# Half of the contraction of three projection groups moved into the start of a diffusion backbone

## The chip, the cores and the metric

The kernel runs on one core of a Trainium2 chip. The metric is the device time of one execution in microseconds (us). The median of three runs of the kernel before is 2949.97 us (2944.76 to 2962.67). A profiled execution, from which every row below comes, took 2949.88 us; its span, from the first to the last instruction of the program, is 2947.9 us.

## The reference, cut to what matters

A two-layer backbone works on 256 latent tokens and 256 context tokens of width 2048, all in float32. Only the beginning of the first layer concerns us:

```
sh1, sc1, ... = split(silu(c) @ ada_w[0] + ada_b[0], 6)          # the same with c_ctx for the context
h  = rmsnorm(x)   * norm_mix[0] * (1 + sc1)  + sh1               # 256 x 2048, "modulation"
hc = rmsnorm(ctx) * norm_mix[0] * (1 + csc1) + csh1
ka, va, kb, vb, a, b, qa, qb, za = split(h  @ ev_w_in[0])        # input projection
ka, va, kb, vb, a, b            = split(hc @ ev_w_in[0])         # context: the first six alone
ka, va, qa = silu(short convolution over tokens, 5 taps)
y = [ gated delta rule(qa, ka, va, a, b, za) , neighbourhood attention(qb, kb, vb) ] @ ev_w_out[0]
x = x + g1 * y
```

The gated delta rule (GDN) splits time into chunks of 64, solves a small triangular system in each, and carries a state over the chunks: first over the context, then over the latent tokens. After it come the feed-forward part of layer 0, a layer with a short gated convolution, and its feed-forward part. `ka`, `va` and `qa` are 1024 columns wide each.

## The kernel before, in words

**Precision.** Each weight tile `raw` is split into `whi` (rounded, on ScalarE) and `wlo` (the rest; 576 of 1024 columns on VectorE, the others on GpSimd). The activations are split in the same way, and each product is three matmuls: hi x hi, lo x hi, hi x lo.

**Streams.** `fm_stream` computes 512 columns of the projection as four groups `f` of 128 columns, for the latent (256) and the context (256) tokens, in four PSUM banks; it goes over the 16 blocks `k` of the contraction (128 each). One step is one `k`: for each `f`, three products for each of the two token sets, 24 matmuls of 256 columns. In the very first step two of them are joined to one of 512 columns, from a tile `h0` in which latent and context lie side by side. Weights come two `k` at a time, 512 KB per DMA from SyncE's queue (`load_w`, L230); four raw tiles and two pairs of split tiles rotate. `grouped` holds back the matmuls of the last two steps (`TAIL`) so that each `f` ends, and is evacuated, while the next still runs. Seen as a generator, a stream gives control back after each step.

**The start.** The shift and the scale of the first modulation take 33.5 MB of `ada_w`. They come in eight blocks `b` of 256 columns (`start_block`: four DMAs of 1 MB in eight issues, 16 products with the conditioning vector, L484). `start_tokens(b)` copies the result (`mrow`, L490), turns it (L495), forms shift and scale, transposes the normalised tokens (L192), modulates (L508), and splits into `h_hi`, `h_lo` (L509, L510) for `k` = 2b and 2b+1. After each of the first seven blocks two steps of the first stream are traced: columns 0 to 511 of `ka`, called KA0 here. It has its last two steps after the eighth block.

**What follows.** KA1 (`ka` 512 to 1023), the gates (a, b), the chunk matrices and the triangular solve of the context, QA0 and QA1, VA0 and VA1, then the scans over the context and the latent tokens, with the streams of `qb`, `kb`, `vb` and `za`, neighbourhood attention, and the output projection (WO). Evacuating a KA, VA or QA stream (`head_evac`) copies the four sums to `hst` tiles (four buffers), and queues the convolution of each `f` (`conv_silu`: ScalarE and four taps on VectorE, L563), the transposes and the norm as work that later steps pop, one item per step (`later`, `drive`). The result goes to DRAM (`kd` by L630) and is read by the GDN part.

**Other vectors.** A `Pump` feeds the remaining `ada_w` products of layer 0 (`ada_job`, 192 steps of 256 KB, L330 and L338) between the steps of the streams: one per KA1 step, 0.5 per QA, 0.8 per VA, 0.6 per QB, 1.3 per KB, VB and ZA, 1.0 per WO step. Sixteen steps make a block of 512 columns, twelve blocks three vectors; a block's products are added up on VectorE (three of four) and on ScalarE and GpSimd, then summed over the partitions by TensorE in a small PSUM tile (L345). The last of them, the scale `sc` of the feed-forward part (L363), is used by the norm after WO (L1185).

**Order.** The program is traced in this order, but a planner places the instructions on each engine when the program is built: it simulates the time line and lets an instruction that is ready go ahead of one that was traced earlier and isn't. On the chip each engine then follows its list, and SyncE's queue is a list too.

Of the kernel before, what the change touches and what calls it, by code (L numbers as in the profile page):

```python
# [26 lines left out]
OP = mybir.AluOpType  # L27
# [3 lines left out]
KT = D // 128  # L31
FH = 5632
# [77 lines left out]
def body(tc, x, c, ctx, c_ctx, ada_w, ada_b, norm_mix, norm_ffn, ffn_w_gate, ffn_w_up, ffn_w_down,  # L110
# [186 lines left out]
    def fm_stream(segs, ks, ws, evac, cut=None):  # L297

        ps = [None] * 4
        for i, group in grouped(((k, (k, hi, lo)) for k, hi, lo in w_steps(segs, ks, cut)), len(ks)):  # L300
            for f in range(4):
                if i == 0:
                    ps[f] = mmt()
                for g, (k, hi, lo) in enumerate(group):
                    a, b = hi[:, f * 128:(f + 1) * 128], lo[:, f * 128:(f + 1) * 128]
                    if i == 0:
                        PE.matmul(ps[f][:, 0:len(ws) * 256], a, h0[:, 0:len(ws) * 256], start=True, stop=False)
                    for j, (wt, mv) in enumerate(((a, h_hi), (a, h_lo), (b, h_hi))):
                        for n, w in enumerate(ws):
                            if j or i:  # L310
                                PE.matmul(ps[f][:, n * 256:(n + 1) * 256], wt, mv(w, k), start=False,  # L311
                                          stop=i == len(ks) - 1 and g == len(group) - 1 and j == 2 and w == ws[-1])
                if i == len(ks) - 1:
                    evac(f, ps[f])
            yield
# [108 lines left out]
    h0 = hlp.tile([128, 512], F32R, name="h0")  # L424
    hs_hi = (hlp.tile([128, KT - 1, 256], F32R, name="hlhi"), hcp.tile([128, KT - 1, 256], F32R, name="hchi"))
    hs_lo = (hlp.tile([128, KT, 256], F32R, name="hllo"), hcp.tile([128, KT, 256], F32R, name="hclo"))

    def h_hi(w, k):
        return hs_hi[w][:, k - 1, :] if k else h0[:, w * 256:(w + 1) * 256]
# [8 lines left out]

    st = Stack()
# [48 lines left out]
    def start_tokens(b, pr):  # L488
        mrow = sp.tile([128, 512], F32, name="mrow", tag="mrow", bufs=2)
# [12 lines left out]
        for k in range(2 * b, 2 * b + 2):  # L502
# [3 lines left out]
            for w in range(2):  # L506
                m = sp.tile([128, 256], F32, name="modt", tag="modt", bufs=4)
                ACT.activation(m, p[:, w * 256:(w + 1) * 256], AF.Identity, bias=sh0[:, k, w:w + 1], scale=sc0[:, k, w:w + 1])  # L508
                DVE.tensor_copy(h_hi(w, k), m)  # L509
                DVE.tensor_tensor(h_lo(w, k), m, h_hi(w, k), op=OP.subtract)  # L510

    def token_stats():
# [5 lines left out]
        junk = sp.tile([128, D], F32, name="junk")  # L518
# [49 lines left out]
    def head_evac(n, q, c0, done, sums):  # L568
# [58 lines left out]
    def ka_evac(q):  # L627
# [3 lines left out]
        return head_evac(4, q, 0, done, True)  # L631

    def va_evac(q):
        def done(vt, ss):
            ACT.dma_start(hslice(vd_, 0, 4, q), vt.rearrange("p t h e -> p t (h e)"))
        return head_evac(4, q, 8, done, False)
# [25 lines left out]
    rstk = Stack()  # L662
# [13 lines left out]
    drive(fm_stream([(wv, C_KA + 512, 512)], ks, [0, 1], ka_evac(1)), pump, R_KA)  # L676
# [80 lines left out]
    state = gw.tile([128, 2, 8, 128], F32, name="state")  # L757
# [94 lines left out]
    def inverses(parts, q):  # L852
# [7 lines left out]
        xdT = gw.tile([128, 16, 128], F32, name="xdT", tag="xdT", bufs=XDT)  # L860
# [113 lines left out]
    for q in range(2):  # L974
        drive(fm_stream([(wv, C_VA + q * 512, 512)], ks, [0, 1], va_evac(q)), pump, R_VA)
# [50 lines left out]

    for q in range(2):
# [372 lines left out]
```

## Time and profile before

| | |
|---|---|
| median of three runs | 2949.97 us (2944.76 to 2962.67) |
| profiled execution, its span | 2949.88 us, 2947.9 us |
| TensorE (PE) busy, mean granted clock | 2764.4 us (94%), 0.978 |
| VectorE (DVE) busy | 1901.8 us (65%) |
| ScalarE (ACT) busy | 1337.0 us (45%) |
| GpSimd (POOL) busy | 596.2 us (20%) |
| read and written in HBM | 657.63 MB and 20.48 MB |

The page gives each engine's busy time, and its share of each of 40 equal slices of the span. A view by windows gives the same for stretches that the reader names, each number with the count of instructions in brackets, then the clock that was granted to TensorE, the busy share of the DMA engines and what they moved. The time line lists instructions as start, duration, engine, line, operation, output<-inputs, with the idle time of the engine ahead of it and what ended that in square brackets. A matmul's end is modelled: the pace is read from the distance between the starts of two of them.

### The profile page before, as it was taken

How to read it: one execution, taken by the hardware profiler on the slowest of the kernel's cores; microseconds unless marked ns; L12 is line 12 of the kernel's file. 1: busy time of each engine (PE TensorE's matmuls, PEld its weight loads, DVE VectorE, ACT ScalarE, POOL GpSimd, SP SyncE). 2: the span in 40 equal slices, each digit the busy share in tenths (PEclk: the TensorE clock that was granted, in tenths of full speed). 3: DMA queues.
4: the chain of work that ended last, by engine and by line, in shares of the span. 5: the costliest groups of instructions: out<-in, count | busy, mean ns of one | idle time of the engine just before them, and what ended most of it. 6: DMA issues, size and time to landing. Idle time of an engine off the chain costs nothing. (4 is left out here: it accounts for less than half of the span.)

```text
span 2947.9 us, 40712 instructions
## 1 busy us (share of the span) xinstructions
PE 2764.4 (94%) x15113; PEld 2295.6 (78%) x15113; DVE 1901.8 (65%) x2409; ACT 1337.0 (45%) x1822; POOL 596.2 (20%) x431
## 2 busy tenths in 40 slices
PE   6998888989899899999999998899999999999997
PEld 3697888978777778888878777777778888888886
DVE  2378786744457777666777767777767546445675
ACT  3245444333355444544445555344454444444554
POOL 1157535335241111100111101111111001000010
PEclk9998999999999999999999999999999999999999
DMA  9955657765657688877778766878658657656553
GB/s 343 289 162 160 185 177 251 232 205 184 180 155 262 236 298 294 293 266 270 268 273 274 252 204 234 285 268 297 211 177 315 199 184 257 188 182 220 192 192 123
DMA packets 284930, 680.82 MB, mean 231 GB/s; under 512 B 57273, under 2 KB 97313, under 8 KB 283323
## 3 DMA queue, kind: packets, MB, share of 16 engines
q1 hardware_dynamic: 262148, 652.48, 66.6%
q10 hardware_dynamic: 22583, 25.73, 2.9%
q8 instruction: 119, 1.95, 0.3%
q14 instruction: 80, 0.66, 0.1%
HBM read 657.63 MB, written 20.48 MB: 230 GB/s over the span
## 5 line engine op out<-in xcount | busy, mean ns | idle before, releaser
L241 DVE TENSOR_TENSOR wlo<-raw,whi 128x1024 fp32r<-128x1024 f32 (+1 forms) x800 | 998.0, 1260 | 530.7 <-ACT whi L173 499.2
L173 ACT ACTIVATE whi<-raw 128x1024 fp32r<-128x1024 f32 x800 | 835.8, 1056 | 668.0 <-PE mm L285 479.4
L338 DVE SCALAR_TENSOR_TENSOR acc<-araw,cT,acc 128x1024 f32<-128x1024 f32 (+1 forms) x312 | 366.5, 1175 | 248.7 <-DMA araw<-in_ada_w_dram 222.3
L283 PE MATMUL mm<-wlo,fhi 128*128 128x512 f32 x1232 | 477.7, 393 | 2.1 <-DVE wlo L241 2.0
L282 PE MATMUL mm<-whi,fhi 128*128 128x512 f32 x1232 | 475.9, 397 | 0.0
L285 PE MATMUL mm<-whi,flo 128*128 128x512 f32 x1232 | 392.4, 392 | 0.0
L336 POOL TENSOR_TENSOR acc<-araw,acc 128x1024 f32<-128x1024 f32 (+1 forms) x78 | 159.0, 2039 | 1068.6 <-ACT araw L335 599.5
L283 PEld LDWEIGHTS mm<-wlo,fhi 128*128 128x128 f32 x1232 | 232.4, 189 | 53.7 <-DVE wlo L241 5.0
L285 PEld LDWEIGHTS mm<-whi,flo 128*128 128x128 f32 x1232 | 231.6, 188 | 50.6
L282 PEld LDWEIGHTS mm<-whi,fhi 128*128 128x128 f32 x1232 | 232.7, 189 | 48.4
L282 PE MATMUL mm<-whi,ahi 128*128 128x512 f32 x672 | 262.3, 395 | 4.0 <-DVE rtmp L1157 2.9
L283 PE MATMUL mm<-wlo,ahi 128*128 128x512 f32 x672 | 261.9, 393 | 0.2 <-DVE wlo L241 0.2
L243 POOL TENSOR_TENSOR wlo<-raw,whi 128x448 fp32r<-128x448 f32 x112 | 163.4, 1460 | 285.7 <-ACT whi L173 267.3
L285 PE MATMUL mm<-whi,alo 128*128 128x512 f32 x672 | 211.7, 395 | 2.8 <-DVE alo L177 2.6
L335 ACT ACTIVATE araw<-araw,cT 128x1024 f32<-128x1024 f32 (+1 forms) x78 | 74.4, 954 | 256.3 <-DMA araw<-in_ada_w_dram 235.2
L311 PE MATMUL mm<-hllo,whi 128*128 128x256 f32 x640 | 184.1, 293 | 0.0
L311 PE MATMUL mm<-hlhi,wlo 128*128 128x256 f32 x600 | 168.3, 296 | 14.1 <-DVE wlo L241 10.6
L311 PE MATMUL mm<-hlhi,whi 128*128 128x256 f32 x600 | 170.4, 296 | 5.8 <-ACT whi L173 4.2
L1159 POOL TENSOR_TENSOR xs<-rtmp,xs 128x512 f32<-128x512 f32 x24 | 35.4, 1493 | 633.2 <-DVE rtmp L1157 631.9
L282 PEld LDWEIGHTS mm<-whi,ahi 128*128 128x128 f32 x672 | 127.0, 189 | 32.9 <-issue 3.4
L285 PEld LDWEIGHTS mm<-whi,alo 128*128 128x128 f32 x672 | 126.2, 189 | 32.7 <-DVE alo L177 5.7
L283 PEld LDWEIGHTS mm<-wlo,ahi 128*128 128x128 f32 x672 | 126.8, 189 | 29.5 <-DVE wlo L241 2.0
(398 smaller groups left out, 4694.0 us busy)
## 6 DMA issues: line engine op xcount, KB each, us to landing
araw<-in_ada_w_dram SPq DMA_DIRECT2D x288, 512.0 KB
raw<-in_ffn_w_down_dram SPq DMA_DIRECT2D x176, 512.0 KB
raw<-in_ffn_w_gate_dram SPq DMA_DIRECT2D x160, 512.0 KB
raw<-in_ffn_w_up_dram SPq DMA_DIRECT2D x160, 512.0 KB
raw<-in_ev_w_in_dram SPq DMA_DIRECT2D x112, 512.0 KB
araw<-in_ada_w_dram SPq DMA_DIRECT2D x192, 256.0 KB
raw<-in_od_w_in_dram SPq DMA_DIRECT2D x96, 512.0 KB
raw<-in_ev_w_out_dram SPq DMA_DIRECT2D x32, 512.0 KB
```

Source lines behind the costliest of these rows:

```text
L173: ACT.activation(dst, src, AF.Copy)
L241: DVE.tensor_tensor(lo[:, 0:cut], raw[:, 0:cut], hi[:, 0:cut], op=OP.subtract)
L243: POOL.tensor_tensor(lo[:, cut:], raw[:, cut:], hi[:, cut:], op=OP.subtract)
L282: PE.matmul(ps[ti][n], a, hi[:, n * 512:(n + 1) * 512], start=first, stop=False)
L283: PE.matmul(ps[ti][n], a, lo[:, n * 512:(n + 1) * 512], start=False, stop=False)
L285: PE.matmul(ps[ti][n], b, hi[:, n * 512:(n + 1) * 512], start=False, stop=last)
L311: PE.matmul(ps[f][:, n * 256:(n + 1) * 256], wt, mv(w, k), start=False, stop=i == len(ks) - 1 and g == len(group) - 1 and j == 2 and w == ...
L335: ACT.activation(raw, raw, AF.Copy, scale=col)
L336: POOL.tensor_tensor(acc2, raw, acc2, op=OP.add)
L338: DVE.scalar_tensor_tensor(acc, raw, col, acc, op0=OP.mult, op1=OP.add)
L1159: eng.tensor_tensor(v, tmp, v, op=OP.add)
```

## The change

Three streams are cut in two along the contraction: the first eight `k`, and the last eight. VA0's first half and KA1's first half (`half`) are traced in the start, ahead of KA0. Their sums are copied from PSUM to two SBUF tiles `part` (2 x 1 MB, 8 KB of a partition each); when the second half has run, `head_evac` adds `part` on VectorE in place of the copy. KA0 keeps its 16 steps in one accumulation. Of the three streams 24 steps are traced in the blocks 0 to 6, as 2, 2, 2, 6, 4, 4 and 4, where KA0 had 14 as 2 each; KA0 has eight steps after the eighth block, KA1 and VA0 eight each in their old places.

The two `part` tiles take the places of `state` and of one `xdT` buffer of the GDN part, whose pool (`xp`) now opens before the start. To make room, `mrow` has one buffer in place of two, `modt` three in place of four, and `junk` lies in `hs_lo`. A second tile in which latent and context lie side by side (`lead[8]`) serves the first step of the second halves.

```diff
@@ fm_stream
-                        PE.matmul(ps[f][:, 0:len(ws) * 256], a, h0[:, 0:len(ws) * 256], start=True, stop=False)
+                        PE.matmul(ps[f][:, 0:len(ws) * 256], a, lead[k][:, 0:len(ws) * 256], start=True, stop=False)
...
-    h0 = hlp.tile([128, 512], F32R, name="h0")
+    lead = {k: hlp.tile([128, 512], F32R, name=f"h{k}") for k in (0, KH)}      # KH = 8
...
+    rstk = Stack()
+    xp = pool("sums", stack=rstk, side="right")
...
-        mrow = sp.tile([128, 512], F32, name="mrow", tag="mrow", bufs=2)
+        mrow = sp.tile([128, 512], F32, name="mrow", tag="mrow", bufs=1)
...
-                m = sp.tile([128, 256], F32, name="modt", tag="modt", bufs=4)
+                m = sp.tile([128, 256], F32, name="modt", tag="modt", bufs=3)
...
-        junk = sp.tile([128, D], F32, name="junk")
+        junk = hs_lo[0][:, 0:KH, :].rearrange("p k t -> p (k t)")
...
@@ head_evac
-            copy(st_[i_], p[:, 0:n * 128])
+            if part is None:
+                copy(st_[i_], p[:, 0:n * 128])
+            else:
+                DVE.tensor_tensor(st_[i_], p, part[:, i_, :], op=OP.add)
...
+    def half(c0, tag, **kw):
+        part = xp.tile([128, 4, 512], F32, name="part", tag=tag, **kw)
+        return part, fm_stream([(wv, c0, 512)], ks[:KH], [0, 1], lambda f, p: copy(part[:, f, :], p))
...
+    part_va, sv_ = half(C_VA, "state")
+    part_ka, sk_ = half(C_KA + 512, "xdT", bufs=XDT)
     s0 = fm_stream([(wv, C_KA, 512)], ks, [0, 1], ka_evac(0))
+    plan = [s for s, n in ((sv_, KH), (sk_, KH), (s0, KH)) for _ in range(n)]
     for b in range(8):
         start_tokens(b, sums)
         if b < 7:
-            next(s0), next(s0)
+            for _ in range((2, 2, 2, 6, 4, 4, 4)[b]):
+                next(plan.pop(0))
             sums = start_block(b + 1)
+    for s in plan:
+        next(s)
...
-    drive(fm_stream([(wv, C_KA + 512, 512)], ks, [0, 1], ka_evac(1)), pump, R_KA)
+    drive(fm_stream([(wv, C_KA + 512, 512)], ks[KH:], [0, 1], ka_evac(1, part_ka)), pump, R_KA)
...
-    for q in range(2):
-        drive(fm_stream([(wv, C_VA + q * 512, 512)], ks, [0, 1], va_evac(q)), pump, R_VA)
+    drive(fm_stream([(wv, C_VA, 512)], ks[KH:], [0, 1], va_evac(0, part_va)), pump, R_VA)
+    drive(fm_stream([(wv, C_VA + 512, 512)], ks, [0, 1], va_evac(1)), pump, R_VA)
```

More of the change, by code (lines that the diff above doesn't have):

```diff
@@ L31 @@
 KT = D // 128
+KH = KT // 2
 FH = 5632
@@ L566, in conv_silu, with head_evac @@
         return o
-    def head_evac(n, q, c0, done, sums):
+    def head_evac(n, q, c0, done, sums, part=None):
         st_ = {}
@@ L756, in body @@
     flush()
-    state = gw.tile([128, 2, 8, 128], F32, name="state")
     def g4(name, tag, bufs=1):
```

18 lines of the change are left out of this document (10 added, 8 removed).

## The prediction

> **What bounds the kernel now.** I read the page first, for the share of TensorE and for the slices in which it is not full.
>
> ```profile
> PE 2764.4 (94%) x15113; PEld 2295.6 (78%) x15113; DVE 1901.8 (65%) x2409; ACT 1337.0 (45%) x1822; POOL 596.2 (20%) x431
> ...
> PE   6998888989899899999999998899999999999997
> ```
>
> TensorE is busy 94% of the span, so the same work placed elsewhere gains only what idle time, or half-speed time, it fills. One slice is 74 us. The first is thin, and slices 4 to 10 (220 to 740 us) are at 8 as often as at 9. The view by windows, cut where a block of the start turns (L495) and where the first matmuls of KA1 (146.10), QA0 (204.40) and QB0 (406.70) stand, says what is thin there.
>
> ```profile
> 44.57:80.03 35.46, 32.89 (x257) 23.43 (x253) 11.21 (x32) 7.03 (x11) 5.12 (x3) 1.00 1.09 353
> 80.03:136.83 56.80, 51.68 (x385) 35.50 (x385) 17.71 (x52) 12.17 (x20) 7.74 (x6) 0.94 0.95 309
> 136.83:146.10 9.27, 8.10 (x64) 7.61 (x65) 4.28 (x13) 3.37 (x7) 3.03 (x2) 1.00 0.66 172
> 146.10:204.40 58.30, 55.86 (x462) 54.69 (x461) 47.99 (x59) 24.98 (x34) 36.86 (x29) 1.00 0.49 150
> 204.40:300.00 95.60, 81.47 (x592) 78.54 (x591) 79.15 (x140) 51.66 (x80) 61.90 (x55) 0.89 0.52 165
> 300.00:406.70 106.70, 96.44 (x773) 94.40 (x773) 90.76 (x171) 45.84 (x72) 55.50 (x57) 0.97 0.55 165
> ```
>
> The columns are window, length, then busy time of PE, its weight loads, DVE, ACT and POOL, the granted clock, the share of the DMA engines and GB/s. In the start (rows one to three) the DMA engines are full, at 353 GB/s, and TensorE is nearly full as well: 51.68 of 56.80 us from the turn of block 3 (80.03) to that of block 7 (136.83). The three rows after are KA1, then QA with the first GDN matrices, then VA with the triangular solve. There VectorE is busy 217.9 of 260.6 us, and TensorE idles 2.4, 14.1 and 10.3 us. So the start, where the change works, has little room, and the stage from which it takes work has more holes.
>
> The time line of TensorE shows the holes of the start themselves.
>
> ```profile
> 82.33 1.06 PE L484 MATMUL gd<-araw,cT 128*32 128x512 f32 x8 [0.23 <-DMA araw<-in_ada_w_dram]
> 88.92 0.28 PE L311 MATMUL mm<-hlhi,wlo 128*128 128x256 f32 x1
> 89.04 0.28 PE L311 MATMUL mm<-hchi,wlo 128*128 128x256 f32 x1
> 92.44 1.07 PE L484 MATMUL gd<-araw,cT 128*32 128x512 f32 x8 [1.27 <-DMA araw<-in_ada_w_dram]
> 94.42 1.84 PE L495 MATMUL sm<-cs,mrow 128*128 128x2 f32 x8 [0.91 <-DVE mrow L490]
> 97.14 1.94 PE L484 MATMUL gd<-araw,cT 128*32 128x512 f32 x8
> 136.83 1.02 PE L495 MATMUL sm<-cs,mrow 128*128 128x2 f32 x8 [0.91 <-DVE mrow L490]
> 137.71 1.18 PE L192 MATMUL sm<-cs,xn 128*128 128x128 f32 x8
> 140.06 0.74 PE L311 MATMUL mm<-hlhi,whi 128*128 128x256 f32 x4 [1.17 <-DVE hlhi L509]
> ```
>
> A projection matmul starts 0.12 us after the one before (88.92, 89.04), so one step of 24 is 2.88 us. TensorE waits 0.91 us in each block for the copy of `mrow`, now and then for `ada_w`, and 1.17 us for the last modulation: at these points KA0 has nothing left that is ready. Shortly after the two waits near 92 us the pace halves: eight L484 take 1.94 us in place of 1.06.
>
> ```profile
> 90.26:100.77 10.51, 8.34 (x48) 4.56 (x38) 3.19 (x9) 1.57 (x4) 1.70 (x1) 0.69 1.09 352
> 80.03:136.83 56.80, 25.31 (x192) 23.99 (x192) 0.94 0.95 309
> L484 PE MATMUL gd<-araw,cT 128*32 128x512 f32 x128 | 17.9, 629 | 1.5 <-DMA araw<-in_ada_w_dram 1.5
> L495 PE MATMUL sm<-cs,mrow 128*128 128x2 f32 x33 | 5.2, 274 | 4.5 <-DVE mrow L490 4.5
> ```
>
> The clock granted there was 0.69. The second row is the same window for L311 alone. At full pace the stretch would need 192 x 0.12 = 23.0 us of projection, 16 groups of L484 at 1.06 = 17.0, four of L495 at 1.02 = 4.1 and four of L192 at 1.18 = 4.7, in sum 48.8. It took 56.8. The loss of 8.0 us is 5.1 idle (the two waits above are nearly all of it) and 2.9 of slow clock; with the 1.17 at 140.06 there are **9.2 us to win in the start**, and no more.
>
> **The change part by part.**
>
> *Steps moved forward.* The first three blocks keep two steps each. The other blocks get ten steps more than before: 10 x 2.88 = **28.8 us** of TensorE are added before the end of the start, and the same is missing from KA1 and VA0 (eight each, less six that KA0 has left over). Where TensorE sets the pace on both sides this sums to nothing. Blocks 3 to 6 then need 48.8 + 28.8 = 77.6 us. The DMA engines need less: 27 issues of `ada_w` and the old weights took the 56.8 us, five more weight loads of 0.52 MB at 353 GB/s are 7.4 us. So TensorE takes over as the bound, and waits for `ada_w` should vanish. SyncE's queue gets those five L230 issues ahead of L481 issues of the next block; three of them, 4.5 us, stand ahead of block 4, behind 17.3 us of matmuls.
>
> *Holes filled.* A partial sum needs only `k` below 8, long ready in blocks 4 to 6, and KA0's `k` 8 to 13 are ready while the last modulation is under way. I take 7 of the 9.2 us: half of the four `mrow` waits (1.8 us) stays, since the planner places by its own durations. Bounds: nothing, and 9.2. Below nothing only if a moved load makes TensorE wait, which the 17.3 us rule out.
>
> By the Trainium skill ("TensorE: Matmul & The Clock Gate", Part 1: The HAM clock gate), half speed follows a whole idle window of some 3.4 us. The trace has no such gap near 92 us, with 1.07 us of matmuls between the waits, and still shows the drop, so the trace doesn't bear the rule out here. By the rule the 2.9 us would have another cause and stay, and the gain would be about 4.
>
> *Sums parked and added back.*
>
> ```profile
> 144.98 0.69 DVE L170 COPY hst<-mm 128x512 f32<-128x512 f32 x1 [2.78 <-PE mm L311]
> 144.62 0.60 ACT L168 ACTIVATE hst<-mm 128x512 f32<-128x512 f32 x1 [4.26 <-PE mm L311]
> L1157 DVE TENSOR_TENSOR rtmp<-mm,row x8: 673/678/685, 939.9 to 994.0; 128x512 f32<-128x512 f32 x8
> L241 DVE TENSOR_TENSOR wlo<-raw,whi 128x576 fp32r<-128x576 f32 x40 | 41.3, 1032 | 14.8 <-ACT whi L173 14.6
> L241 DVE TENSOR_TENSOR wlo<-raw,whi 128x576 fp32r<-128x576 f32 x4 | 3.0, 759 | 23.8 <-ACT whi L173 23.8
> L338 DVE SCALAR_TENSOR_TENSOR acc<-araw,cT,acc 128x512 f32<-128x512 f32 x36 | 35.8, 994 | 3.5 <-DMA araw<-in_ada_w_dram 3.2 <-DMA acc<-in_ada_b_dram 0.3
> ```
>
> Eight copies to `part` are 4 x 0.69 on VectorE and 4 x 0.60 on ScalarE, in a stretch where these are busy 17.7 and 12.2 of 56.8 us: hidden behind the projection of the next stream, whose first group comes three groups (4.3 us) after the bank's last. Without that cover it is 0.7 us per change of stream. Later eight additions of PSUM and SBUF, 0.68 each (L1157), stand for four copies of 0.69 and four on ScalarE: VectorE +2.7 us. Five split halves move out of the dense stage (1.03 each between 146 and 406 us, 0.76 in the start): −5.2. The two extra joined first steps replace 8 x 2 starts of 0.12 by 8 of 0.24: nothing.
>
> *Pump.* 8 fewer `ada` steps go with KA1 and 0.8 x 8 = 6.4 with VA0. Three of four are an L338, so VectorE loses 14.4 x 0.75 x 0.994 = 10.7 us between 146 and 406. They come later, and where they end matters.
>
> ```profile
> 752.92 0.33 SPq L330 DMA_DIRECT2D araw<-in_ada_w_dram  x1
> 906.30 0.95 PE L345 MATMUL sm<-cs,acc 128*128 128x1 f32 x8
> 916.87 0.33 SPq L330 DMA_DIRECT2D araw<-in_ada_w_dram  x1
> 993.90 0.14 DVE L363 SCALAR_TENSOR_TENSOR sc<-sm,vecT 128x4 f32<-128x4 f32 x1
> L1185 ACT ACTIVATE modt<-sm,sh,sc x16: 546/564/572, 1001.5 to 1013.4; 128x256 f32<-128x256 f32 x16
> ```
>
> The pump stands still from 752.9 to 916.9: a block of 16 steps is summed (L345) only after the attention heads, whose PSUM slots come first in the trace. The last result is there at 993.9, used at 1001.5: 7.6 us to spare. By VB's end 160 steps are traced before (ten blocks of 16), 145.6 after (just over nine). The tenth block can then load in the standstill and be summed where it is now, and the last two run in WO as now: I take nothing. If instead the 14.4 steps follow at the end, at 2.7 us each (28 loads from 916.9 on, ended by 993.9), they are 39 us, less 7.6: **31 us** is the other bound.
>
> *Buffers.* `mrow` alone: its next copy is a block later. The fourth `modt` of a block waits for the first's readers, 0.29 + 0.42 of VectorE against 1.45 us of three activations: nothing; at the worst 0.3 us in each of eight blocks. `junk` and `lead` change addresses. `state` and `xdT` are needed hundreds of us after their `part` is read.
>
> *Sum.* 2949.9 − 7 = **2943 us**. The median stands 0.1 us from the profiled time, so it serves for both.
>
> **The rivals.**
>
> *VectorE becomes the bound in the dense stage (slower).* Block 7 turns at 136.83 + 28.8 − 7 = 158.6. From there to the end of VA, VectorE had 4.28 + 217.9 = 222.2 us in 269.9 (82%); it will have 222.2 − 5.2 − 10.7 + 2.7 = 209.0, and in my forecast 241.1 us for it (87%). If it can't go above 82%, VA ends at 158.6 + 254 = 412.5, 5.8 later than now: **2956**. For it: two convolutions come closer together and GpSimd is full beside them; the same split takes 0.76 or 1.03. Against: slices of this stage show 9. The Trainium skill ("SBUF — State Buffer", Who interferes with whom) says that VectorE with two SBUF inputs and GpSimd lock each other out of a port; the two durations agree.
>
> *The GDN chain ends last (slower).* KA0's sums now end after sixteen more steps, at 146.1 + 46.1 − 7 = 185, KA1's at 204.4 + 23 − 7 = 220.
>
> ```profile
> 204.82 0.63 ACTq L630 DMA_DIRECT2D kd<-hq  x1
> 297.03 0.54 ACTq L630 DMA_DIRECT2D kd<-hq  x1
> 868.06 0.17 DVE L221 SCALAR_TENSOR_TENSOR ror<-ros,ror 128x8 f32<-128x8 f32 x1
> 886.54 0.53 SPq L779 DMA_DIRECT2D vtok<-zd  x1
> 895.21 2.18 DVE L1018 SCALAR_TENSOR_TENSOR o_t<-o_t,ror,vtok 128x128 f32<-128x128 f32 x8
> ```
>
> From sums to `kd` KA0 took 58.7 us, KA1 92.6. The GDN result is normed by 868.1 but used at 895.2, after the load of `zd` (886.5) that the last stream fills: the chain has 27 us to spare. With KA1's 92.6 from 220, its `kd` comes 16 later, within that. If the two convolutions run strictly one after the other, it comes at 185 + 58.7 + 92.6 = 336, 39 late, 12 beyond the slack: **2962**. It decides from a second `kd` write after 324.
>
> *The pump ends last (slower).* Its 31 us, less the 7 won: **2974**. It decides from a last `sc` after 1001.5, once the planner puts the traced WO steps' weights ahead of `ada_w` in SyncE's queue: 26 of the 32 steps in WO are then traced with a pump step that must run, in place of 11. Against: the 164 us of standstill can hold the missing 14 steps.
>
> *Nothing is filled (the change doesn't do what it says).* The planner may put the extra steps after, not into, the waits: **2950**. For it: TensorE in the start is 91% busy already.
>
> *The dense stage loosens too (faster).* With fewer splits and pump steps there, half of the 14.1 + 10.3 us idle goes as well: 2949.9 − 7 − 12 = **2931**. Against: it takes away matmuls that filled time between GDN steps.
>
> **How the numbers follow.** Forecast 0.38, with its own range 2938 to 2948; nothing filled 0.18; VectorE 0.10; chain 0.08; pump 0.10; looser stage 0.16. The 80% range reaches to 2966 above, short of the pump's whole price, and to 2925 below, for a looser stage with a little more. 1% is 29.5 us, about what a measurement of this kernel can tell from no change; all cases lie inside it, and only the tails of the outer ones leave: faster 0.06, same 0.87, slower 0.07.
>
> **What would show it.** The turn of block 7 near 159 us with TensorE above 95% busy from 80 on, no wait for `ada_w`, clock 1.00; KA0's sums near 185; the second `kd` before 324; VA's end near 400; the pump's last `sc` some 7 us ahead of L1185. The prediction is wrong if TensorE idles more than 27 us between KA0's sums and VA's end, or if `vtok` waits for GDN rather than `zd`.

## The result: 16 us slower, ratio 1.0051

| | before | changed |
|---|---|---|
| median of 20 runs each | 2950.30 us (2941.43 to 2962.67) | 2966.03 us (2957.34 to 2976.62) |
| ratio | | 1.0051 [1.0040, 1.0062] |
| profiled execution, span | 2947.9 us | 2955.1 us |

The forecast was 2943 (2925 to 2966). The change is within 1%, the case that had 0.87, but on the other side of the kernel before, and at the very end of the range. The interval is 0.2% wide, so this kernel's time can be told much finer than the 1% that the forecast took for it. The profiled execution of the changed kernel is one of its quickest (2957.5 us). The difference of the medians is close to the one that the two traces show ahead of the first feed-forward layer, 17.9 us at the first `modt` of `norm_h` (1019.4 for 1001.5). Behind it the stretch between the last two `norm_h` (from the first `modt` of one to that of the next) took 394.8 us, against 403.4 before; over all kernels below it lies between 394.0 and 403.4, with no relation to the edits.

Lines after the start are 1 to 21 further down in the changed kernel: L495 is L501, L560/563/565 of the convolution are L566/569/571, L311 is L312, L338 is L339, L630 is L640, L635 is L645, L363 is L364, L1185 is L1206. L584 is the new addition.

First the steps that the forecast named as its signs, from the time line of the changed kernel (start, duration, engine, line, operation):

```profile
158.75 0.95 PE L501 MATMUL sm<-cs,mrow 128*128 128x2 f32 x8
185.46 0.68 DVE L171 COPY hst<-mm 128x512 f32<-128x512 f32 x1
318.59 0.54 ACTq L640 DMA_DIRECT2D kd<-hq  x1
421.04 0.68 DVE L171 COPY hst<-mm 128x512 f32<-128x512 f32 x1
456.42 0.55 ACTq L645 DMA_DIRECT2D vd__143<-hq  x1
908.32 0.53 SPq L799 DMA_DIRECT2D vtok<-zd  x1
1005.94 0.15 DVE L364 SCALAR_TENSOR_TENSOR sc<-sm,vecT 128x4 f32<-128x4 f32 x1
```

and, by the view of one tile, the `modt` of `norm_h` that the last `sc` feeds:

```profile
L1206 ACT ACTIVATE modt<-sm,sh,sc x16: 555/564/593, 1019.4 to 1029.3; 128x256 f32<-128x256 f32 x16
```

Block 7 turns at 158.75 (forecast 158.6), KA0's last sum leaves its bank at 185.5 (185), the second `kd` write is at 318.6 (before 324), the pump's last `sc` lies 13.5 us ahead of its use. Only VA's end is far off. The forecast read it at the first matmul of QB0, 406.7 in the kernel before, and put it at 400; that matmul now starts at 408.2. But it no longer marks the end of VA: VA's last sum leaves its bank at 421.0, against 409.1 before (its time line):

```profile
409.07 0.68 DVE L170 COPY hst<-mm 128x512 f32<-128x512 f32 x1
```

So VA ends 12.0 us later than before, in place of some 7 earlier. The forecast's own sign of being wrong is there too: between KA0's last sum (185.5) and QB0's first matmul (408.2) TensorE idles 38.7 us, where 27 was the limit.

Then the windows of the kernel before, cut at the end of block 7's turn, the last `vd` write, and the end of `zd` (window, length, busy time of PE, its weight loads, DVE, ACT and POOL, granted clock, DMA share, GB/s). From here on the first window is called the dense stage:

```profile
137.85:439.62 301.77, 264.58 (x2243) 255.98 (x2243) 248.80 (x413) 141.69 (x215) 166.63 (x151) 0.95 0.55 169
439.62:882.11 442.49, 405.64 (x3253) 358.47 (x3249) 242.76 (x447) 168.94 (x316) 188.32 (x154) 0.96 0.66 202
```

and of the changed kernel, with the later part of its start as the first row:

```profile
80.40:158.80 78.40, 78.40 (x644) 65.45 (x644) 25.16 (x61) 19.68 (x29) 17.23 (x10) 1.00 0.82 265
159.70:456.42 296.72, 243.81 (x2104) 233.88 (x2105) 238.59 (x404) 135.15 (x208) 150.56 (x144) 0.90 0.52 157
456.42:900.82 444.40, 402.59 (x3142) 356.02 (x3128) 253.73 (x459) 175.77 (x322) 186.86 (x155) 0.97 0.68 205
```

The account of the 17.9 us: the turn ends 21.85 later (159.70 − 137.85), the dense stage is 5.05 shorter, the next stage 1.91 longer, the stretch from `zd` to `norm_h` 0.8 shorter. The start did what was forecast: 28.8 us of TensorE went in for 21.85 us of time, TensorE is busy 78.40 of 78.40 us, and the clock is 1.00. The dense stage gave 5 of the 28.8 back. TensorE has 20.8 us less to do there by its busy time (and the clock fell from 0.95 to 0.90, so that the same work counts for more), but idles 52.9 us in place of 37.2. One trace of each stands behind this: in the edits below that leave the start alone, the turn ends between 134.5 and 139.6 us on the kernel before and between 158.6 and 161.6 on the changed one. Between their middle values, 136.0 and 159.2, lie 23.2 us, which makes the gain of the start 5.6 us in place of 6.95.

What it waits for, in the view of waits for TensorE over the same window, before (who waited for what: us in total, times, longest):

```profile
PE mm L311 <- DVE wlo L241: 6.9, 5, 2.2
PE sm L192 <- ACT cv L565: 6.3, 8, 1.4
PE sm L192 <- DVE hq L617: 4.1, 2, 3.5
...
PE mm L307 <- DVE hst L170: 2.8, 2, 2.0
```

and in the changed kernel:

```profile
PE sm L193 <- ACT cv L571: 15.1, 10, 2.9
PE mm L312 <- DVE wlo L242: 9.6, 5, 3.6
PE gd L903 <- DMA xd<-dz: 6.8, 2, 5.7
PE mm L308 <- DVE hst L171: 6.4, 3, 5.4
PE sm L193 <- DVE hq L627: 5.4, 4, 2.0
```

The longest row is the end of the convolution: VectorE's four taps (L569), ScalarE's Silu (L571), then TensorE's transposes (L193), which can't start before. The first matmul of a stream (L308) waits for VectorE to empty a bank. In both rows TensorE is ready and VectorE or ScalarE is not. The row of `xd` is a transfer behind the triangular solve; a like wait (L883, 3.4 us) falls in the next stage in the kernel before, so not all of the 15.7 us more idle time comes from the convolution.

The windows of the kernel before had held a warning (columns as above):

```profile
260.00:280.00 20.00, 15.20 (x102) 14.55 (x102) 19.53 (x20) 7.67 (x12) 18.08 (x16) 0.83 0.54 175
360.00:380.00 20.00, 15.01 (x102) 14.62 (x103) 19.62 (x30) 3.94 (x5) 13.47 (x11) 0.83 0.46 135
```

VectorE's 82% over the stage are an average. In these two stretches it is busy 98%, while TensorE idles 4.8 and 5.0 of 20 us: when TensorE's work is taken away there, VectorE has no time left to go faster. The forecast took high slices for a sign that VectorE can do more than 82%.

The long waits cost clock as well. The time line of the changed kernel at the longest of the waits for a bank, and the windows behind it:

```profile
307.53 0.77 PE L308 MATMUL mm<-h,whi 128*128 128x512 f32 x1 [5.37 <-DVE hst L171]
```

```profile
307.50:316.00 8.50, 8.47 (x56) 8.27 (x57) 5.81 (x8) 1.80 (x3) 5.37 (x7) 0.82 0.69 231
316.00:330.00 14.00, 14.00 (x120) 14.00 (x119) 9.97 (x18) 4.81 (x7) 10.31 (x10) 1.00 0.84 282
```

After 5.37 us without a matmul the granted clock is 0.82 over the next 8.5 us, and 1.00 after that: the starts of projection matmuls lie 0.21 us apart until 310.4, and 0.12 from then on. By these starts such a wait costs some 1.4 us more than its own length (an estimate). The Trainium skill ("TensorE: Matmul & The Clock Gate", Part 1: The HAM clock gate) has half speed follow an idle window of about 3.4 us; the trace agrees here.

### The profile page after: what moved, and what is told of

Same layout as the page of the kernel before. It is cut to its first block, busy times and chain, and to the rows that moved or that the text cites. A ratio compares the mean times of both kernels' runs of the same rounds, so it can differ in the third digit from the quotient of the medians.

```text
span 2955.1 us, 40688 instructions
## 1 busy us (share of the span) xinstructions
PE 2762.6 (93%) x15105; PEld 2302.1 (78%) x15105; DVE 1906.7 (65%) x2417; ACT 1342.6 (45%) x1825; POOL 588.1 (20%) x431
## 5 line engine op out<-in xcount | busy, mean ns | idle before, releaser
L242 DVE TENSOR_TENSOR wlo<-raw,whi 128x1024 fp32r<-128x1024 f32 (+1 forms) x800 | 1000.3, 1263 | 491.6 <-ACT whi L174 483.1
L339 DVE SCALAR_TENSOR_TENSOR acc<-araw,cT,acc 128x1024 f32<-128x1024 f32 (+1 forms) x312 | 360.8, 1156 | 277.6 <-DMA araw<-in_ada_w_dram 245.6
L312 PE MATMUL mm<-hllo,whi 128*128 128x256 f32 x640 | 185.8, 295 | 0.0
L312 PE MATMUL mm<-hlhi,wlo 128*128 128x256 f32 x560 | 155.9, 298 | 11.2 <-DVE wlo L242 8.4
L312 PE MATMUL mm<-hlhi,whi 128*128 128x256 f32 x560 | 160.9, 296 | 4.3 <-ACT whi L174 3.8
```

The lines of the kernel that those rows point to most:

```text
L242: DVE.tensor_tensor(lo[:, 0:cut], raw[:, 0:cut], hi[:, 0:cut], op=OP.subtract)
L339: DVE.scalar_tensor_tensor(acc, raw, col, acc, op0=OP.mult, op1=OP.add)
```

## The experiments

The theory at first: once TensorE work leaves the dense stage, it is paced by VectorE and what hangs on it. The rivals: the pump's missing steps are the cause; one of the two parked halves is. From the ninth run on there is one more, the planner's order: any edit draws another order of the instructions, and the kernel before has a good one. (Where the expectations number their theories, the numbers are those of the same run.)

All were timed in five rounds beside the kernel before. The table gathers them, with what the windows of each profile show. The dense stage can hold more or less of the neighbouring work, as the planner puts it, so the columns to compare are the idle ones. The traces are of one execution each, which can lie some us off the median (e5's 7.6 above, e16's 13.5 below).

| kernel | median us | ratio [95%] | dense stage | TensorE idle in it | clock | VectorE busy | next stage | TensorE idle in it |
|---|---|---|---|---|---|---|---|---|
| before | 2950.3 | 1 | 301.8 | 37.2 | 0.95 | 248.8 | 442.5 | 36.9 |
| e9 buffers | 2951.5 | 0.9998 [.9984, 1.0011] | 300.2 | 38.0 | 0.96 | 249.3 | 446.7 | 40.0 |
| e10 R_QA 0.55 | 2970.2 | 1.0059 [1.0037, 1.0080] | 306.3 | 35.5 | 0.95 | 254.5 | 460.3 | 51.3 |
| e12 R_VA 0.9 | 2956.9 | 1.0013 [1.0000, 1.0026] | 309.8 | 36.8 | 0.95 | 257.9 | 441.1 | 45.3 |
| e8 pump late | 2963.5 | 1.0039 [1.0022, 1.0056] | 305.2 | 35.6 | 0.93 | 240.8 | 449.0 | 48.9 |
| e18 pump to ScalarE/GpSimd | 2958.8 | 1.0026 [1.0013, 1.0039] | 319.4 | 41.1 | 0.93 | 253.9 | 439.8 | 44.3 |
| e5 no outer taps | 2965.6 | 1.0053 [1.0034, 1.0071] | 298.5 | 39.0 | 0.97 | 219.1 | 460.7 | 50.6 |
| e19 thin | 2951.5 | 1.0002 [.9991, 1.0014] | 310.9 | 53.6 | 0.90 | 261.7 | 436.4 | 46.2 |
| e20 thin, no outer taps | 2937.2 | 0.9956 [.9943, .9968] | 275.3 | 39.9 | 0.93 | 224.3 | 457.4 | 56.4 |
| changed | 2966.0 | 1.0051 [1.0040, 1.0062] | 296.7 | 52.9 | 0.90 | 238.6 | 444.4 | 41.8 |
| e1 KA1 alone | 2966.0 | 1.0064 [1.0043, 1.0086] | 294.4 | 49.4 | 0.96 | 245.4 | 449.9 | 45.9 |
| e2 VA0 alone | 2970.7 | 1.0073 [1.0058, 1.0088] | 295.3 | 45.8 | 0.95 | 240.4 | 448.2 | 44.8 |
| e3 pump kept | 2988.2 | 1.0131 [1.0114, 1.0149] | 303.7 | 56.9 | 0.90 | 254.3 | 448.0 | 48.8 |
| e6 added on GpSimd | 2977.9 | 1.0096 [1.0080, 1.0112] | 303.6 | 56.8 | 0.92 | 245.9 | 448.4 | 44.3 |
| e7 pump late | 2969.6 | 1.0070 [1.0047, 1.0094] | 287.8 | 49.4 | 0.93 | 229.0 | 443.0 | 44.1 |
| e11 R_QA 0.55 | 2978.3 | 1.0086 [1.0072, 1.0099] | 301.9 | 51.5 | 0.89 | 244.7 | 439.0 | 43.6 |
| e17 pump to ScalarE/GpSimd | 2995.2 | 1.0159 [1.0141, 1.0177] | 301.4 | 58.6 | 0.89 | 239.4 | 455.6 | 50.1 |
| e4 no outer taps | 2959.6 | 1.0030 [1.0015, 1.0044] | 262.9 | 34.6 | 0.95 | 210.5 | 472.5 | 57.6 |
| e16 a quarter of KA1 | 2974.8 | 1.0078 [1.0055, 1.0101] | 301.7 | 41.7 | 0.94 | 253.5 | 448.2 | 51.9 |
| e21 half of KB0 | 2948.2 | 1.0002 [.9988, 1.0017] | 302.5 | 39.8 | 0.96 | 248.7 | 415.5 | 38.6 |

The upper part (to e20) stands on the kernel before, the rest on the changed one.

### One half at a time (e1, e2), the pump kept (e3), the addition on GpSimd (e6)

```diff
 e1
-    plan = [s for s, n in ((sv_, KH), (sk_, KH), (s0, KH)) for _ in range(n)]
+    plan = [s for s, n in ((sk_, KH), (s0, 14)) for _ in range(n)]      # in 2,2,2,4,4,4,4; VA0 whole
 e2: the same with sv_; KA1 whole
 e3
-    drive(fm_stream(..., ks[KH:], [0, 1], ka_evac(1, part_ka)), pump, R_KA)
+    drive(fm_stream(..., ks[KH:], [0, 1], ka_evac(1, part_ka)), pump, 2 * R_KA)      # VA0: 2 * R_VA
 e6
-                DVE.tensor_tensor(st_[i_], p, part[:, i_, :], op=OP.add)
+            copy(st_[i_], p[:, 0:n * 128])
+            if part is not None:
+                POOL.tensor_tensor(st_[i_], st_[i_], part[:, i_, :], op=OP.add)
```

> Only KA1's first half is parked; VA0 runs whole, in its old place. The start gets 22 steps (KA1's first eight, then 14 of KA0) as 2, 2, 2, 4, 4, 4, 4, so KA0 ends right behind the start, as before the change. Theory 'VectorE's queue' (the convolutions, evacuations and the solve, now with less TensorE time around them, hold back the PSUM banks): KA0's convolution starts 30 us earlier than in the changed kernel and most of the loss goes, 2943 to 2953 us. Theory 'filler' (VA0's second half is too short to cover the GDN chunk chain): VA0 is whole, so the loss goes altogether, 2943. Theory 'pump' (the modulation steps that are pumped later cost at the end): 8 of the 14.4 shifted steps stay shifted, 2957.

> Only VA0's first half is parked; KA1 runs whole, in its old place. The start again gets 22 steps (VA0's first eight, then 14 of KA0). Theory 'VectorE's queue': KA0's convolution is early and KA1 is long enough to cover it, but VA0's evacuation comes right on QA1's: 2950 to 2960. Theory 'filler': the loss stays, 2962 to 2970. Theory 'pump': 6.4 of 14.4 steps stay shifted, 2955.

> The changed kernel, with two pump steps per step of KA1 and 1.6 per step of VA0, so that each stream feeds as many modulation steps as before the change. Theory 'pump': the loss goes, 2943 to 2950. Theory 'VectorE's queue': VectorE gets 10.7 us back in the dense stage, 2966 to 2975. Theory 'filler': no difference from the changed kernel, 2966.

> The changed kernel, with the sums evacuated as before (ScalarE and VectorE in turn) and the parked halves added afterwards on GpSimd, in place of eight additions on VectorE that free the banks. Theory 'VectorE's queue', in the narrow form that the additions themselves hold the banks: 2955 to 2961. If the additions are only a small part of VectorE's load, or by 'filler' or 'pump': 2964 to 2970.

Measured: 2966.0, 2970.7, 2988.2, 2977.9. e1, e3 and e6 lie above every range that was expected, e2 at the end of one. Each half alone costs as much as both, so it is neither the one nor the other. (By their traces the dense stage ends 7.8 us later than before in e1, 14.0 in e2 and 16.8 in the changed kernel; the rest of e1's and e2's loss arises in the next stage.) The missing pump steps aren't the cause: giving them back costs 22 us more, though taking more of them away gains nothing either (e7 below). The addition on GpSimd frees VectorE of nothing (245.9 us busy) and is 12 us slower; one more pass over `hst` now lies ahead of the convolution.

### VectorE's load taken down, on both kernels (e4, e5, e7, e8)

```diff
 e4 (changed), e5 (before): the convolution without its outer taps
-        for i in (0, 1, 3, 4):
+        for i in (1, 3):
 e7 (changed), e8 (before): pump steps moved behind the dense stage
-R_QA = 0.5, R_VA = 0.8, R_KB = 1.3
+R_QA = 0.25, R_VA = 0.4, R_KB = 1.6
```

> The changed kernel with the two outer taps of each short convolution of the GDN part left out (44 of the VectorE operations on the hst tiles between 176 and 460 us, 0.84 us each by the changed kernel's rows: 37 us of VectorE). To be read against the kernel before with the same left out. Theory 'VectorE sets the length of the stage from KA0's sums to VA1's' (it was busy 84 to 87% of it in the kernel before, the changed kernel and four variants): without this load the moved TensorE work is gained back, and this kernel ends 4 to 10 us ahead of the other, about 2920 to 2935. Theory 'filler, GDN chain': the chain of the chunk matrices lacks cover as before, 10 to 20 us behind the other.

> The kernel before with the same two outer taps left out. Theory 'VectorE': TensorE had 90% of the stage already, so it gains less than the changed kernel does, 2930 to 2942. Theory 'filler': 2935 to 2950, with the changed kernel 10 to 20 us behind.

> The changed kernel with half the pump rate in QA and VA (0.25 and 0.4 per step) and 1.6 in place of 1.3 in KB and VB: 17.6 modulation steps leave the dense stage, some 13 us of VectorE. 14.4 steps more there cost 22 us. Theory 'VectorE': 12 to 22 us less than the changed kernel, 2944 to 2954. If these steps cost only where they collide with KA1's and VA0's halves: 2960 to 2966.

> The kernel before with the same three rates (19 steps leave the dense stage). Theory 'VectorE', if it binds before the change as well: 2935 to 2945. If there TensorE binds: 2948 to 2955.

Measured: 2959.6, 2965.6, 2969.6, 2963.5. The kernels without the outer taps leave out part of the computation. As times all four are misses for the theory that VectorE sets the pace; only the 6 us between e4 and e5 are what it expected. Less work made the kernel *before* 13 to 15 us slower, which VectorE's pace can't explain; that brought up the order as a rival. But the dense stage speaks for VectorE. Windows of e5 and, below, of e4:

```profile
139.57:438.07 298.50, 259.47 (x2168) 249.81 (x2167) 219.11 (x362) 145.12 (x216) 162.29 (x150) 0.97 0.55 168
```

```profile
159.36:422.26 262.90, 228.31 (x1789) 221.75 (x1789) 210.49 (x353) 140.45 (x206) 156.80 (x143) 0.95 0.54 168
```

Without the outer taps, VectorE has 29.7 us less to do in the kernel before, and the stage is only 3.3 us shorter: TensorE paces it. In the changed kernel 28.1 us less make it 33.8 us shorter, TensorE's idle time falls from 52.9 to 34.6, and the clock is back at 0.95. e7 says the same with less: 9.6 us off VectorE, stage 9.0 shorter. It doesn't become a gain: e7's `zd` ends 11.5 us ahead of the changed kernel's, but its `norm_h` starts at 1019.3, for 1019.4. e8 has 8.0 us less on VectorE in this stage, which is 3.4 us longer: before the change VectorE alone doesn't set it.

### Edits that change next to nothing (e9 to e12)

```diff
 e9 (before): mrow bufs=2 -> 1, modt bufs=4 -> 3, junk in hs_lo; nothing parked
 e10 (before), e11 (changed)
-R_QA = 0.5
+R_QA = 0.55
 e12 (before)
-R_VA = 0.8
+R_VA = 0.9
```

> The kernel before with the buffer part of the change alone: one mrow for two, three modt for four, junk in the halves of h_lo; no sum is parked. Theory 1 (the change itself costs its 16 us, in the dense stage, where moved TensorE work isn't won back): no sum is moved, so 2950, within 3. Theory 2 (the order that the planner gives the kernel before is an unusually good one, and any edit draws another): some 2 to 15 us slower, 2952 to 2965; the smaller the fewer instructions change places. Theory 3 (fewer buffers make the start wait, the forecast's worst case of 0.3 us in each of eight blocks): 2952 to 2953, with block 7 turned 2 us later and all behind it as before.

> The kernel before with R_QA 0.55 for 0.5: 0.8 pump steps more in QA0 and QA1 together of 160, some 2 us of work moved earlier. Theory 1 (the change itself costs 16 us): this is no change, 2950 within 3. Theory 2 (a good draw of the planner, lost with any edit): 2955 to 2970.

> The changed kernel with R_QA 0.55 for 0.5. Theory 1: 2966 within 3. Theory 2: another draw from the same lot as the kernel before with an edit, 2955 to 2970, up to 11 us off the changed kernel on either side.

> The kernel before with R_VA 0.9 for 0.8: 1.6 pump steps of 160 more in the V streams of path A, some 4 us of work moved earlier. Theory 1: 2950 within 3. Theory 2: 2955 to 2970.

Measured: 2951.5, 2970.2, 2978.3, 2956.9. The buffer part costs nothing measurable, as the forecast had it. Moving 0.8 pump steps, some 2 us of work, forward cost 20 us on the kernel before and 12 on the changed one. So the order's share is real: by the whole time alone the change's 16 us couldn't be told from it. In e10 most of it lies in the next stage, here by windows:

```profile
440.97:901.24 460.27, 409.00 (x3226) 359.36 (x3225) 250.43 (x464) 172.49 (x325) 187.48 (x156) 0.95 0.67 203
```

Its dense stage ended as before (440.97 against 439.62), and TensorE idled 35.5 us in it. The next stage has 460.27 us with 51.3 idle, against 442.49 with 36.9. Over the six edits of the table on either kernel that do all of the work and leave TensorE's where it was (e8 to e12, e18) this idle time is 40.0 to 51.3: the kernel before has the lowest. The stretch from `zd` to `norm_h` scatters as well, from 112.4 to 130.0 us over all kernels, and e11's loss lies there and in the dense stage. So a single comparison of two orders carries up to some 20 us of luck. In the dense stage the idle time scatters less: 35.5 to 41.1 on the kernel before with all its TensorE work, 45.8 to 58.6 where at least eight steps of KA1 or VA0 were moved and all taps are done.

### TensorE's work taken out without parking (e19), and with the taps out too (e20)

```diff
 e19 (before), streams KA1 and VA0 only (np_=2; leaves the low weights' product out)
-                    for j, (wt, mv) in enumerate(((a, h_hi), (a, h_lo), (b, h_hi))):
+                    for j, (wt, mv) in enumerate(((a, h_hi), (a, h_lo), (b, h_hi))[:np_]):
 e20: e19 and
-        for i in (0, 1, 3, 4):
+        for i in (1, 3):
```

> The kernel before without the third product (low part of the weights by high part of the activations) in the streams KA1 and VA0: 30.7 us of TensorE work leave the stage, nothing is parked, VectorE's work and the start stay. This leaves out part of the computation. Two-bound theory: TensorE's bound falls to 271, VectorE's stays at 249 + 54 = 303, so the stage still lasts some 300 and the time is 2945 to 2955. TensorE theory, on which the forecast stood: the stage shortens by the 30.7 us, 2920. Order theory: 2920 plus 5 to 20.

> Both omissions on the kernel before: no third product in KA1 and VA0 (30.7 us of TensorE), and no outer taps in the convolution (37 us of VectorE). Each alone left the stage from block 7's turn to the last vd write at 311 and 299 us, against 302. This leaves out part of the computation. Chain theory (the stage is the longer of TensorE's pace and the convolution's chain): now both are shorter, the stage lasts 265 to 275, and the time is 28 below that of the kernel without the outer taps (2966): about 2938. Rival (something else, or the planner's order alone, holds the stage near 300): 2955 to 2970.

Measured: 2951.5, ratio 1.0002 [0.9991, 1.0014], and 2937.2. Leaving 30.7 us of TensorE work out of KA1 and VA0 gained nothing. Windows of e19, its largest wait, and the windows of e20:

```profile
135.85:446.73 310.88, 257.24 (x2207) 245.39 (x2207) 261.73 (x417) 152.35 (x227) 169.00 (x156) 0.90 0.58 171
```

```profile
PE sm L192 <- ACT cv L565: 20.4, 11, 5.5
```

```profile
136.10:411.44 275.34, 235.46 (x1795) 228.11 (x1794) 224.32 (x362) 144.13 (x214) 167.77 (x151) 0.93 0.59 179
```

The signature of e19 is that of the changed kernel, with nothing parked and the start untouched: idle 53.6, clock 0.90, and the wait for `cv` up from 6.3 to 20.4. (That wait alone is no mark: it is 14.5 in e5 and 12.8 in e20, whose idle time is 39.0 and 39.9. And e19's stage holds more of the neighbouring work, VectorE 261.7 us for 248.8, so its 311 us are not all its own.) With the convolution lightened, the same omission takes 23.2 us from the dense stage (298.5 to 275.3) and 28.4 from the time (2965.6 to 2937.2, forecast 2938). So both hold the stage: without the one or the other alone it lasts 311 and 299 us, without both 275. Order is an unlikely source of this: e20 carries the longest idle time but one of the next stage (56.4) and is the fastest kernel of all, and 53.6 lies outside what the dense stage scatters by.

### VectorE's work moved to other engines (e17, e18), a smaller part (e16)

```diff
 e17 (changed), e18 (before)
-                elif k % 4 == 1:
+                elif k % 4 == 1 or (width == 512 and k % 4 == 3):
 e16 (changed): KH = KT // 4, KA1 only, in 2,2,2,2,3,3,4
```

> The changed kernel, with half of the pump's steps in layer 0 accumulated by ScalarE and GpSimd in place of a quarter: 12 of the 36 VectorE accumulations of the stage leave it, 11 us. Two-bound theory: VectorE 227 + 54 = 281, TensorE 243 + 37 = 280, so the stage lasts 281 in place of 296 to 297, and the time is 2951. Order theory: 2955 to 2980, with no relation to VectorE's busy time. A shared path of VectorE and GpSimd would show as longer operations on VectorE.

> The same edit on the kernel before. Two-bound theory: VectorE falls by 13 us to 290, TensorE's bound stays at 302, so the stage keeps 302 us, and the time 2950 plus what the order costs later (0 to 20). A theory by which VectorE's waits set both kernels alike: 13 us less, 2937.

> A quarter of KA1's contraction is parked, and nothing of VA0: 4 steps, 11.5 us of TensorE, about the 9.2 us idle and slow in the start. Two-bound theory (the stage from block 7's turn to the last vd write is the longer of TensorE's busy time + 37 and VectorE's + 54): turn at 137.9 + 11.5 - 7 = 142, TensorE bound 290, VectorE bound 245 + 54 = 299, so the last vd write at 441, 1 us later than before: 2951. TensorE theory (the start's 7 us are won and the rest sums to nothing, as forecast): 2943. Order theory (any edit draws another order): 2955 to 2970.

Measured: 2995.2, 2958.8, 2974.8. e17 is a plain miss: 44 us above its forecast. e18's time fits, its stage doesn't: 319.4 us in place of 302, with VectorE at 253.9 in place of some 236: it holds work that else runs in the next stage, where VectorE has 221.2 for 242.8. The dense stage of e17, by its windows, by VectorE's groups (busy us, mean ns of one), and its largest wait:

```profile
159.11:460.54 301.43, 242.86 (x1948) 232.48 (x1947) 239.39 (x393) 139.48 (x214) 169.81 (x156) 0.89 0.52 154
```

```profile
L569 DVE SCALAR_TENSOR_TENSOR cv<-hst,evcT,cv 128x508 f32<-128x508 f32 (+3 forms) x96 | 85.5, 903 | 7.0 <-ACT cv L566 6.2
...
L339 DVE SCALAR_TENSOR_TENSOR acc<-araw,cT,acc 128x512 f32<-128x512 f32 x24 | 27.1, 1129 | 14.5 <-DMA araw<-in_ada_w_dram 14.5
```

```profile
PE sm L193 <- ACT cv L571: 22.9, 11, 5.3
```

against the same groups of the changed kernel:

```profile
L569 DVE SCALAR_TENSOR_TENSOR cv<-hst,evcT,cv 128x508 f32<-128x508 f32 (+3 forms) x96 | 78.8, 836 | 8.7 <-ACT cv L566 8.0
...
L339 DVE SCALAR_TENSOR_TENSOR acc<-araw,cT,acc 128x512 f32<-128x512 f32 x36 | 33.9, 941 | 21.3 <-DMA araw<-in_ada_w_dram 21.3
```

Twelve accumulations left VectorE, but it is as busy as in the changed kernel (239.4 for 238.6): a tap takes 903 ns in place of 836, an accumulation 1129 in place of 941, beside a GpSimd that is busy 169.8 us in place of 150.6. The means alone don't show the reason: over the other kernels with all taps they scatter from 824 to 914 and from 915 to 1065, and the splits of the weights (L242) took 970 in e17 for 1004. Instruction by instruction it shows. In the changed kernel's dense stage a tap of 508 or 510 columns took 740 ns on average where GpSimd did nothing meanwhile (43 of 64), and 1341 where GpSimd was busy for more than half of it (18); in e17 these are 739 (35) and 1485 (23). For the splits of the changed kernel it is 749 (14 of 40) and 1175 (24). The Trainium skill ("SBUF — State Buffer", Who interferes with whom) says that a VectorE instruction with two SBUF inputs contends with a GpSimd instruction that reads SBUF; the durations agree. So the simple form of the theory, in which VectorE's busy time plus a constant is the stage's length, falls as a rule to forecast with. What stays is the chain: its taps, Silu and transposes come later than TensorE can use, and work given to GpSimd or ScalarE didn't shorten it here. e16 has nearly the dense stage that the two-bound theory gives (301.7 us for 299, last `vd` write at 444 for 441). Its trace loses more in the next stage (idle 51.9) and behind it, where the orders scatter; but that execution, 2961.2 us, is 13.5 quicker than e16's median, and of the rest there is no trace.

### The holes filled with work from another stage (e21)

```diff
-    part_ka, sk_ = half(C_KA + 512, "xdT", bufs=XDT)      # of e1
+    part_kb, sk_ = half(C_KB, "xdT", bufs=XDT)            # then SP.dma_start(kbp_d, part)
...
+            SP.dma_start(st_, kbp_d[:, i, :])             # KB0's second half
+            DVE.tensor_tensor(st_, p, st_, op=OP.add)
+            ACT.dma_start(kb_d[:, i, :], st_)
```

> The holes of the start are filled with half of KB0's contraction in place of KA1's and VA0's: 8 steps, 23 us of TensorE. The sums wait in DRAM and are added when KB0's other half ends, in the stage behind the V streams, where no convolution runs. Chain theory: turn of block 7 at 138 + 23 - 7 = 154, the stage up to the last vd write keeps its 302 us, the next one loses 23 us of its 442 us: zd's end at 875 and the time 2943, plus what the new order costs (0 to 20). Rival (what is moved into the start always sums to a loss, wherever it came from): 2960 to 2970, with TensorE idle 15 us more behind the start.

Measured: 2948.2, ratio 1.0002 [0.9988, 1.0017]. The windows of its dense and of its next stage:

```profile
155.52:458.05 302.53, 262.70 (x2233) 253.54 (x2233) 248.69 (x414) 141.60 (x215) 163.56 (x149) 0.96 0.56 169
458.05:873.52 415.47, 376.84 (x3051) 329.94 (x3047) 230.93 (x429) 159.88 (x302) 176.44 (x146) 0.97 0.69 209
```

The dense stage kept its 302.5 us, and the next one gave up 27.0 us for the 23 taken out: as a stage that TensorE paces would have it. `zd` ends at 873.5 (875 expected), 8.6 ahead of the kernel before. Then 6.3 us are lost again on the way to `norm_h` (125.7 us for 119.4), inside the 112.4 to 130.0 by which that stretch scatters, and no run explains it. The kernel isn't measurably faster than the one before, but 18 us faster than the changed one, with the same idea and nearly as long a start as with KA1 alone (155.5 and 153.1). No version that does all of the work beat the kernel before.

## Why the prediction was wrong, step by step

- **The start: right.** 7 us of the 9.2 were taken; measured are 28.8 − 21.85 = 6.95. That it is so close is in part luck: the forecast left half of the `mrow` waits in, and none is left; the 1.17 us at 140.06, also gone, lie behind the point of the turn where this is read; and the turn scatters by some us. (The DMA engines, said to be full in all three rows of the start, are so in the first alone: 353, 309 and 172 GB/s. Nothing hung on it.) TensorE is never idle from 80.40 to 158.80, nothing there waits for `ada_w`, and the clock is 1.00. With the two waits gone the drop of the clock went too, as the forecast read it from the trace before. By the rule of the Trainium skill ("TensorE: Matmul & The Clock Gate", Part 1: The HAM clock gate) that the forecast weighed there, the gain would have been about 4, with the slow clock left in; the clock of 1.00 doesn't bear that out.
- **"28.8 us of TensorE ... sums to nothing": the step that failed.** It stood under "where TensorE sets the pace on both sides". TensorE sets it in the start, and in the dense stage only as long as all its work is there. The two limits were about level in the kernel before, at some 300 us (298.5 with VectorE's work lightened, e5). The term was not 0 but 28.8 − 5.05 = +23.7 us. e19 shows it without the start: 30.7 us of TensorE work taken out of the stage were worth 0, and 28.4 once the convolution was lightened too (e20 against e5). The rows were there: VectorE busy 82% of that stage, 98% in the stretches above, and TensorE with holes. They were read as "more holes", a stage that can spare TensorE work, where idle time of an engine that works through a list says that something it waits for is late.
- **The rival "VectorE becomes the bound": right in kind, too small.** It priced 5.8 us (VA's end at 412.5, 2956) by holding VectorE at 82% from the turn of block 7 to QB0's first matmul, and lowering its work there by 13 us. VectorE was busy 204.4 of these 249.5 us, 82%, as the rival said. What failed is the point at which it stopped counting: QB0's first matmul comes 1.5 us later than before, VA's last sum 12.0, the last `vd` write 16.8. Which link makes the delay grow on this way isn't shown; the convolution's chain (taps, Silu, transposes), the transfer behind the solve, and the clock (0.95 to 0.90) all have a part in the rows. The clock isn't needed for the loss: e1 keeps 0.96, and loses as much. The rival deserved the place of the forecast.
- **Parking and adding, with the pump's steps (−13 us of VectorE, valued at nothing): right in sign.** VectorE's work in the dense stage fell by 10.2 us. The additions take 686 ns each, as the row of L1157 said. What the 10.2 us were worth no run shows by itself; where VectorE's chain holds the stage, they may be the 5.05 us that came back.
- **The pump: right.** Last `sc` 13.5 us ahead of its use; giving the steps back (e3) costs 22 us.
- **The GDN chain: right.** The second `kd` write came at 318.6, and `vtok` is loaded at 908.3, behind `zd`'s end at 900.8.
- **The buffers: right,** shown alone by e9, ratio 0.9998.
- **Not among the steps: the planner.** An edit of 2 us of work can cost 20 us (e10). TensorE's 4.9 us more idle time in the next stage are inside that scatter and say nothing about the change; the 15.7 us in the dense stage lie outside the scatter of that stage.

Open stays which link of the chain ends last (taps, Silu, bank copies; e6 and e17 only show that GpSimd was no relief), why the next stage is 18 to 28 us longer without the outer taps (e5 to before, e4 to changed, e20 to e19), why e7 gains nothing by `norm_h`, and the 6.3 us behind `zd` in e21. A deeper ring of `cv` buffers wasn't tried.

## What to carry to other kernels

Before moving work out of a stage, ask what that stage would be limited by without it: a stage in which TensorE idles 12% while another engine is busy 82% can be held by both, as here, and then taking TensorE's part away gives nothing. Take the work for a hole from a stage that gets shorter by what is taken out (here the streams without a convolution, though that too ended level with the kernel before), and test it cheaply by leaving the work out without parking it. Where a planner writes the order, compare stages by their idle time over several harmless edits before believing a difference below the scatter that these show.

## What the runs showed of the hardware

- A wait of 5.37 us left the clock at 0.82 over the next 8.5 us (changed kernel): matmuls 0.21 us apart for 2.9 us, then 0.12. Over the whole dense stage the clock was 0.90 in the changed kernel with 52.9 us of idle time, but 0.96 in e1 with 49.4: the sum of the idle time doesn't tell it. Nor is one long wait needed: in the kernel before, 0.69 over 10.5 us came with waits of 1.27 and 0.91 us (the windows and the time line in the prediction).
- A VectorE operation with two SBUF inputs took 740 to 749 ns (taps of 508 or 510 columns, splits of 576) when GpSimd was idle, and on average 1341 and 1175 when GpSimd was busy for more than half of it (changed kernel). In e17 more taps fell beside GpSimd (23 of 64 for 18), and VectorE stayed as busy as before with 12 of 36 accumulations gone.
